# A hybrid encoder block whose modulation vectors are all made on the tensor engine in four column groups

## Chip, cores and metric

The kernel runs on one core of one Trainium2 chip. The metric is the device time of one execution in microseconds (us), the median over several runs. All data are float32 in device memory at the start and the end.

## What is computed

One block works on x (1024 tokens of 1024 channels) with a conditioning vector c of 1024 numbers. Six modulation vectors of 1024 numbers each come from c by one matrix:

```
c_act = silu(c)
mod = c_act @ ada_w + ada_b                      # 1024 x 6144
sh1, sc1, g1, sh2, sc2, g2 = split(mod, 6)
h = rmsnorm(x, norm1_g) * (1 + sc1) + sh1
p = h @ w_in                                     # S5 input, Hyena input, two sigmoid gates
merged = gate_a * (s5(p) @ w_branch_a) + gate_b * (hyena(p) @ w_branch_b)
x = x + g1 * (merged @ w_out)
h = rmsnorm(x, norm2_g) * (1 + sc2) + sh2
x = x + g2 * swiglu_ffn(h)
out = rmsnorm(x, final_g)
```

The S5 branch is a bidirectional scan over 32 groups; the Hyena branch makes two long convolutions with filters that a small network generates. The matrix `ada_w` has 1024 rows, which are the sum's index: eight tiles of 128 rows (partitions). It is 25 MB, the largest single weight that gives only a vector.

## The kernel before, in words

Python loops write out every instruction, and a scheduler then sets each engine's order once, from a model of the times: what comes earlier in the text has priority, and an instruction that is ready later is put behind others on its engine. On the chip every engine works through its list in that order and waits at semaphores. All loads and stores but a few go through one queue, that of SyncE (SP), in order too. Tiles come from pools; tiles with the same tag share a number of rooms (`bufs`), and a new tile waits until the older one in its room has been read for the last time.

The stages, with the time of the profiled execution:

- 0 to 50 us: constants, x (eight tiles of 128 tokens) and the first two vectors' part of `ada_w` (eight blocks of 1024 rows by 256 columns, `load_ada1`) are loaded; sums of squares (`emit_stats1`), the filter network (`emit_mlp`) and the vectors of the first norm (`emit_mod1`, L1080) are made. The order `ADA1 = (4, 0, 5, 1, 6, 2, 7, 3)` takes blocks of sc1 (4 to 7) and sh1 (0 to 3) by turns. A block of sc1 goes to PE: eight products with one column of silu(c) as the stationary operand and 128 x 256 of the weights moving (L1104), a float32 product being two passes in the trace, then a copy of one row (L1105). A block of sh1 is multiplied by silu(c) per partition and added over the eight row tiles: for one block on ACT and POOL (L1093, L1095), for three on DVE (L1097, L1099). What is left, a sum over 128 partitions, is made by 16 small products with ones (L1109, L1110), which also turn the row into columns (`E.mod`).
- 50 to 90 us: the normalised x is turned and modulated (`emit_norm1`: L1148 or L1150 makes a tile `hk`, L135 rounds it, L136 subtracts for the low part). The tag `hk` has two rooms, which the tiles `tt` of the turned convolutions (`emit_turn`, L1208) use as well.
- 57 to 345 us: the Hyena filters (`emit_filters`, four passes; L243 and L244 on PE, L247 on ACT, L250 and L255 on DVE, L256 on POOL), beside the projections of four convolution tiles (`emit_conv`, `proj`: each loads 512 KB of weights, ACT rounds, POOL subtracts, PE makes three products for each one of float32), the S5 inputs (`emit_u`) and later convolutions. Each pass loads one row `hb` (L227) that is added once (L252); it has a room of its own.
- In the same stretch `emit_ada` (L950) makes three more chunks of 1024 columns: 2 (g1), 4 (sc2) and 3 (sh2), each in two halves of 512 columns. For each half eight loads of 128 x 512 (256 KB) come through three rooms of a tile with tag `ax`; the first and the even tiles are multiplied and added on DVE (L962, L967), the odd ones are multiplied on ACT (L964) and added on POOL (L965). The bias row of chunk 2 is added on DVE (L972). The 128 partial sums go to device memory (`E.acc`, L973). The tag `ax` is used before by x tiles and after by a scratch tile of the S5 scan (`beside`).
- 345 to 640 us: S5 parameters and scan (`emit_s5`; L798, L877 on DVE, L807, L819, L856, L881 on PE), with the projections of the gates between. Then the GLU, the two long convolutions (to 900 us), the merge (`emit_merge`, to 965 us).
- In the merge `emit_ada_end` (L983) loads the partial sums back and adds over the partitions on PE: with ones on all columns where a vector is wanted along the free side (L992, g1 and g2), or turned to columns (`mod_columns`).
- 965 to 1080 us: the output projection (`emit_out`). After its first quarter of the second half of tokens, `between()` runs `last_gate`: chunk 5 (g2) by the same `emit_ada`, with two rooms for loads, and its `emit_ada_end`.
- to 1835 us: the feed-forward part, nearly all on PE; g2 is used there (L1417).

Of the kernel before, what the change touches and what calls it, by code (L numbers as in the profile page):

```python
# [15 lines left out]
L = 1024  # L16
# [139 lines left out]
def col(ap, i):  # L156
    return ap[:, i:i + 1]
# [45 lines left out]
def emit_filters(E):  # L203
    nc, d = E.nc, E.d
    sp = lambda: ps.tile([P, 2, 256], F32, tag="sp", name="sp", bufs=3)
    with ExitStack() as ctx:
        fp = ctx.enter_context(E.tc.tile_pool(name="flt", bufs=1, reuse_waits="tile"))
        ps = ctx.enter_context(E.tc.tile_pool(name="flt_ps", bufs=2, space=PSUM, reuse_waits="tile"))
        for o in range(2):
            for hf in range(2):  # L210
# [1 line left out]
                w3 = fp.tile([P, 2, 256], F32, tag="w3", name="w3")  # L212
                wd = fp.tile([P, 2, 256], F32, tag="fbt", name="wd", bufs=2)
                dec = fp.tile([P, 2, 256], F32, tag="dec", name="dec")
                hb = fp.tile([1, 256], F32, tag="hb", name="hb")
                col0 = o * 1024 + 256 * hf
                for s in range(2):
                    c = slice(col0 + 512 * s, col0 + 512 * s + 256)
# [519 lines left out]
def emit_s5(E, before):  # L738
# [5 lines left out]
    with ExitStack() as ctx:  # L744
# [1 line left out]
        ps = ctx.enter_context(E.tc.tile_pool(name="s5_ps", bufs=1, space=PSUM, reuse_waits="tile"))  # L746
        cs = op.tile([P, 8], F32, name="cs2")
        nc.scalar.activation(out=cs, in_=E.pf[:, PF_C:PF_C + 8], func=ACTF.Silu)
        nc.vector.tensor_copy(E.cs, cs)
        j8 = op.tile([P, 1, P], F32, name="j8")  # L750
        nc.sync.dma_start(out=j8[:, 0], in_=d["c_j8"])
        with E.tc.tile_pool(name="s5p", bufs=1, reuse_waits="tile") as pp:
# [183 lines left out]
def emit_setup(E, cp):  # L936

    nc = E.nc
    E.pf, E.pk = (cp.tile([P, n], F32, name=f"pk{n}") for n in (11, P))
    for rows, out in zip(E.rows, (E.pf, E.pk)):  # L940
        n = rows.shape[0]
        pt = E.mm.tile([P, n], F32, tag="mm", name="pkp")
        nc.tensor.transpose(pt, rows, E.ident[0:n, 0:n])
        nc.vector.tensor_copy(out, pt)
    E.cs = cp.tile([P, 8], F32, name="cs")
    nc.scalar.activation(out=E.cs, in_=E.pf[:, PF_C:PF_C + 8], func=ACTF.Silu)
    E.mod = cp.tile([P, 4, 8], F32, name="mod")


def emit_ada(E, chunks, sums, loads):  # L950


    nc = E.nc
    for q in chunks:
        for hf in range(2):
            acc = sums()
            for k in range(8):
                w = loads()
                c0 = L * q + 512 * hf
                nc.sync.dma_start(out=w, in_=E.d["ada_w"][0, P * k:P * k + P, c0:c0 + 512])  # L960
                if k == 0:
                    nc.vector.tensor_scalar(out=acc, in0=w, scalar1=col(E.cs, 0), scalar2=None, op0=ALU.mult)  # L962
                elif k % 2:
                    nc.scalar.mul(w, w, col(E.cs, k))  # L964
                    nc.gpsimd.tensor_tensor(out=acc, in0=acc, in1=w, op=ALU.add)  # L965
                else:
                    nc.vector.scalar_tensor_tensor(out=acc, in0=w, scalar=col(E.cs, k), in1=acc,  # L967
                                                   op0=ALU.mult, op1=ALU.add)
            if q in (2, 5):
                b = loads()[0:1]  # L970
                nc.sync.dma_start(out=b, in_=E.d["ada_b"][:, L * q + 512 * hf:L * q + 512 * hf + 512])
                nc.vector.tensor_tensor(out=acc[0:1], in0=acc[0:1], in1=b, op=ALU.add)  # L972
            nc.sync.dma_start(out=E.acc[q - 2, :, 512 * hf:512 * hf + 512], in_=acc)  # L973


def ada_rooms(E):

    t = [E.dft.tile([P, 4, 512], F32, tag="ax", name="ada")]
    loads = (t[0][:, 1 + i % 3] for i in range(1000))
    return lambda: t[0][:, 0], lambda: next(loads)  # L980


def emit_ada_end(E, psum, chunks, room):  # L983
# [95 lines left out]

def emit_mod1(E, ap, ps, blocks):  # L1080


    nc = E.nc
    V = nc.vector
    acc = ap.tile([P, L], F32, name="shacc")
    row = ap.tile([1, L], F32, name="scrow")
    for n, c in enumerate(ADA1):
        w = blocks[n]
        r = slice(256 * (c % 4), 256 * (c % 4) + 256)
        if c < 4:  # L1090
            for k in range(8):
                if n < 2:
                    nc.scalar.mul(w(k) if k else acc[:, r], w(k), col(E.cs, k))  # L1093
                    if k:
                        nc.gpsimd.tensor_tensor(out=acc[:, r], in0=acc[:, r], in1=w(k), op=ALU.add)  # L1095
                elif k == 0:
                    V.tensor_scalar(out=acc[:, r], in0=w(0), scalar1=col(E.cs, 0), scalar2=None, op0=ALU.mult)  # L1097
                else:
                    V.scalar_tensor_tensor(out=acc[:, r], in0=w(k), scalar=col(E.cs, k), in1=acc[:, r],  # L1099
                                           op0=ALU.mult, op1=ALU.add)  # L1100
        else:
            pt = ps.tile([1, 256], F32, tag="mrow", name="mrow")
            for k in range(8):
                nc.tensor.matmul(out=pt, lhsT=col(E.cs, k), rhs=w(k), start=k == 0, stop=k == 7)  # L1104
            nc.scalar.copy(row[:, r], pt)  # L1105
    pt = ps.tile([P, 16], F32, tag="mcol", name="mcol")
    for i in range(8):
        c = slice(P * i, P * i + P)
        nc.tensor.matmul(out=pt[:, i:i + 1], lhsT=acc[:, c], rhs=E.ones[:, 0:1], start=True, stop=True)  # L1109
        nc.tensor.matmul(out=pt[:, 8 + i:9 + i], lhsT=row[:, c], rhs=E.ones[0:1, 0:1], start=True, stop=True)  # L1110
    V.tensor_tensor(out=E.mod[:, 0:2].rearrange("p a b -> p (a b)"), in0=pt, in1=E.pk[:, PK_ADA:PK_ADA + 16], op=ALU.add)
    V.scalar_tensor_tensor(out=E.mod[:, 1], in0=E.mod[:, 1], scalar=1.0, in1=E.pk[:, PK_N1:PK_N1 + 8],
                           op0=ALU.add, op1=ALU.mult)
# [371 lines left out]
def hybrid_block(tc, d):  # L1485
# [4 lines left out]
    with ExitStack() as top:  # L1490
# [14 lines left out]
        with ExitStack() as s0:  # L1505
            E.h0 = pool(s0, "h0")
            E.dft = pool(s1, "dft")
            with ExitStack() as s2:
                E.cv = pool(s2, "cv")
                E.mm = pool(s2, "mmB", bufs=3, space=PSUM)  # L1510
                E.h1 = pool(s2, "h1")
                s3 = ExitStack()
                hhp = pool(s3, "hhp", side="right")
                E.hid, E.hid1 = (hhp.tile([P, 2, L], F32R, name=n) for n in ("hid", "hid1"))
                with ExitStack() as s4:
                    ada1 = pool(s4, "ada1", side="right")
                    mlp = pool(s4, "mlp", side="right")
                    ps = pool(s4, "st_ps", space=PSUM)
                    emit_consts(E, E.cp)
                    load_setup(E, mlp)  # L1520
                    E.x8, E.r1 = [], []
                    load_x1(E, range(4))
                    blocks = [load_ada1(E, ada1, n) for n in range(8)]
                    load_x1(E, range(4, 8))
                    emit_setup(E, E.cp)
                    for th in range(2):
                        emit_stats1(E, th)
                    emit_mlp(E, mlp, ps)
                    emit_mod1(E, ada1, ps, blocks)
                    emit_norm1(E)  # L1530
                emit_dft(E, E.cp)
                emit_filters(E)
                s3.close()
                for ct in range(4):
                    emit_conv(E, ct)
                emit_ada(E, (2, 4, 3), *ada_rooms(E))
                emit_s5(E, lambda: [emit_u(E, ct) for ct in range(4)])
                for ct in range(4, 12):
                    emit_conv(E, ct)
                emit_gates_a(E)  # L1540
                emit_glu(E)
            with ExitStack() as s2:
                E.gp = pool(s2, "gp")
                mm = pool(s2, "mmC", bufs=2, space=PSUM)
                emit_hyena(E, lambda: [emit_gates_b(E, mm), emit_branch_a(E, mm)])
            s1.close()
            mm = pool(top, "mmD", bufs=2, space=PSUM)
            pool(top, "edge", side="right").tile([P, 8], F32, name="edge")
            E.actT = pool(top, "actT", bufs=38, side="right")
            xp = pool(top, "x1", side="right")  # L1550
            rows = pool(top, "rows", side="right")
            E.g1, E.g2 = (rows.tile([P, L], F32, name=n) for n in ("g1", "g2"))
            woA = pool(wo, "woA", side="right")
            room = lambda t: xp.tile([P, L], F32, tag=f"x{t}", name="x1")
            x1 = [room(t) for t in range(4)]
            emit_merge(E, mm, x1, lambda c: c in (2, 4, 6) and
                       emit_ada_end(E, mm, ((2, 4, 3)[c // 2 - 1],), lambda n: room(3 + c // 2)))
        with ExitStack() as s0:
            ada2 = pool(s0, "ada2")
            x1 += [room(t) for t in range(4, 8)]  # L1560
            def last_gate():
                emit_ada(E, (5,), lambda: ada2.tile([P, 512], F32, tag="acc", name="acc"),
                         lambda: ada2.tile([P, 512], F32, tag="aw", name="aw", bufs=2))
                emit_ada_end(E, mm, (5,), lambda n: ada2.tile([P, L], F32, name="row"))
            emit_out(E, mm, x1, woA, last_gate)
        wo.close()
# [33 lines left out]
```

## Time and profile before

| | us |
|---|---|
| median of 3 runs | 1838.48 |
| lowest and highest run | 1837.70 and 1839.58 |
| the profiled execution | 1837.27 |
| its span, first to last instruction | 1835.5 |

The profiled execution is 1.77 us longer than its span (start and end of the program). Engines: PE multiplies, PEld loads its stationary operand, DVE is VectorE, ACT ScalarE, POOL GpSimd, SP the queue that issues transfers. A row of a group gives line, engine, operation, output and inputs by the program's names, shapes, count, then busy time in us and the mean of one in ns, then the idle time of the engine just before these instructions and what ended it. A row of waits gives who waited for whom, the sum in us, how often, and the longest.

### The profile page before, as it was taken

The numbers are of one execution on the slowest core, as the hardware profiler recorded it, in microseconds if no ns is written. First come the engines' busy times: TensorE is split into PE (matmuls) and PEld (weight loads), VectorE is DVE, ScalarE is ACT, GpSimd is POOL, SyncE is SP. The second block draws the span as 40 slices with busy tenths as digits, with TensorE's granted clock in tenths as the row PEclk, the third lists the DMA queues.
The fourth block names the chain that finished last, engine by engine and source line by source line (L and its number), as shares of the span: only waits on it lengthen the run. The fifth ranks groups of instructions, "written<-read, shape, count | busy, mean of one in ns | idle before, by whom it ended". The sixth has DMA issues, their size and how long they took to land.

```text
span 1835.5 us, 23003 instructions
## 1 busy us (share of the span) xinstructions
PE 1657.1 (90%) x8700; PEld 1401.9 (76%) x8700; DVE 1066.4 (58%) x1548; ACT 593.2 (32%) x1037; POOL 749.4 (41%) x509
## 2 busy tenths in 40 slices
PE   6778888987777898988699999999999999999996
PEld 2667777876666776767579978899888988899885
DVE  6889789779999637888877741123111321124127
ACT  5855454443333254122234531111111111110125
POOL 2356545258775347688511221212221222222234
PEclk9988999999888999999799999999999999999998
DMA  9446733523221357743277311111111111112112
GB/s 325 119 130 180 215 97 97 167 76 89 58 78 57 90 167 263 244 155 115 81 231 237 118 41 46 46 41 53 47 53 39 47 58 46 40 36 63 47 52 92
DMA packets 212946, 194.38 MB, mean 106 GB/s; under 512 B 23783, under 2 KB 174143, under 8 KB 211395
## 3 DMA queue, kind: packets, MB, share of 16 engines
q1 hardware_dynamic: 212356, 190.50, 33.7%
q0 software_dynamic: 480, 2.42, 0.4%
q8 instruction: 68, 1.11, 0.3%
q14 instruction: 42, 0.34, 0.1%
HBM read 149.91 MB, written 42.96 MB: 105 GB/s over the span
## 4 chain that ended last, share of the span: by engine, by line
PE 44%; DVE 3%; DMA 2%; ACT 1%; issue 0%; POOL 0%; ACTq 0%; SPq 0%; DVEq 0%; POOLq 0%
PE gu L144 9%; PE gu L146 9%; PE gu L145 9%; PE dn L146 4%; PE dn L144 4%; PE dn L145 4%; DMA wof<-in_w_out_dram 1%; PE wop L146 1%; PE wop L144 1%; PE wop L145 1%; PE br L144 1%; PE br L145 1%; PE br L146 1%; DVE x L1418 0%; DMA acc<-acc 0%
## 5 line engine op out<-in xcount | busy, mean ns | idle before, releaser
L136 POOL TENSOR_TENSOR wl<-wf,wh 128x1024 fp32r<-128x1024 f32 (+1 forms) x126 | 286.2, 2272 | 707.3 <-ACT wh L135 654.9
L135 ACT CAST wh<-wf 128x1024 fp32r<-128x1024 f32 (+1 forms) x126 | 118.3, 939 | 616.5 <-issue 196.2
L144 PE MATMUL gu<-h2T,wh 128*128 128x512 f32 x704 | 277.5, 396 | 3.4 <-ACT silu L1432 2.8
L145 PE MATMUL gu<-h2T,wh 128*128 128x512 f32 x704 | 278.6, 396 | 0.0
L146 PE MATMUL gu<-h2T,wl 128*128 128x512 f32 x704 | 278.4, 396 | 0.0
L1433 DVE TENSOR_TENSOR silu<-gu,silu 128x1024 f32<-128x1024 f32 x22 | 27.0, 1225 | 383.7 <-PE gu L146 377.3
L144 PE MATMUL pj<-hT,wh 128*128 128x512 f32 x480 | 196.5, 409 | 8.8 <-ACT cva L1180 8.1
L146 PE MATMUL pj<-hT,wl 128*128 128x512 f32 x480 | 195.0, 406 | 3.3 <-POOL wl L136 3.3
L146 PE MATMUL dn<-wh,act 128*128 128x256 f32 x576 | 162.6, 283 | 0.0
L145 PE MATMUL dn<-wl,act 128*128 128x256 f32 x576 | 162.6, 283 | 0.0
L144 PE MATMUL dn<-wh,act 128*128 128x256 f32 x576 | 161.5, 283 | 0.0
L144 PEld LDWEIGHTS gu<-h2T,wh 128*128 128x128 f32 x704 | 132.8, 189 | 35.2 <-ACT silu L1432 3.2
L146 PEld LDWEIGHTS gu<-h2T,wl 128*128 128x128 f32 x704 | 132.9, 189 | 31.2
L145 PEld LDWEIGHTS gu<-h2T,wh 128*128 128x128 f32 x704 | 133.0, 189 | 31.1
L144 PEld LDWEIGHTS pj<-hT,wh 128*128 128x128 f32 x480 | 94.9, 198 | 28.3 <-ACT cva L1180 8.8
L1417 DVE TENSOR_TENSOR tmp<-dn,g 128x256 f32<-128x256 f32 x96 | 36.0, 416 | 134.6 <-PE dn L146 134.6
L146 PEld LDWEIGHTS pj<-hT,wl 128*128 128x128 f32 x480 | 94.2, 196 | 23.0 <-POOL wl L136 4.2
L145 PEld LDWEIGHTS dn<-wl,act 128*128 128x128 f32 x576 | 110.6, 192 | 0.1
L146 PEld LDWEIGHTS dn<-wh,act 128*128 128x128 f32 x576 | 110.6, 192 | 0.0
L144 PEld LDWEIGHTS dn<-wh,act 128*128 128x128 f32 x576 | 109.9, 192 | 0.1
L145 PE MATMUL pj<-hT,wh 128*128 128x512 f32 x256 | 104.5, 408 | 0.0
L145 PE MATMUL pj<-lT,wh 128*128 128x512 f32 x224 | 90.1, 402 | 0.0
(411 smaller groups left out, 3733.8 us busy)
## 6 DMA issues: line engine op xcount, KB each, us to landing
wf<-in_ffn_w_gu_dram SPq DMA_DIRECT2D x44, 512.0 KB
wf<-in_w_in_dram SPq DMA_DIRECT2D x36, 512.0 KB
ada<-in_ada_w_dram SPq DMA_DIRECT2D x48, 256.0 KB
x<-in_x_dram SPq DMA_DIRECT2D x16, 512.0 KB
kt<-kspec SPq DMA_DIRECT2D x32, 256.0 KB
wof<-in_w_out_dram SPq DMA_DIRECT2D x16, 512.0 KB
wf<-in_ffn_w_down_dram SPq DMA_DIRECT2D x16, 512.0 KB
kspec<-kt SPq DMA_DIRECT2D x28, 256.0 KB
```

The lines of the kernel that those rows point to most:

```text
L135: E.nc.scalar.copy(hi, src)
L136: (lo_eng or E.nc.vector).tensor_tensor(out=lo, in0=src, in1=bc(hi), op=ALU.subtract)
L144: E.nc.tensor.matmul(out=out, lhsT=lh, rhs=rh, start=first, stop=False, skip_group_check=shared)
L145: E.nc.tensor.matmul(out=out, lhsT=lh, rhs=rl, start=False, stop=False, skip_group_check=shared)
L146: E.nc.tensor.matmul(out=out, lhsT=ll, rhs=rh, start=False, stop=last, skip_group_check=shared)
L1417: V.tensor_tensor(out=tmp, in0=acc, in1=E.g2[:, cs], op=ALU.mult)
L1433: V.tensor_tensor(out=s, in0=pts[1], in1=s, op=ALU.mult)
```

## The change

All chunks go through one function. `E.csx` holds silu(c) with 31 columns of zeros behind each of its eight columns, so that a stationary operand is 32 columns wide; the product with row tile k goes to partitions 32 (k mod 4) onwards of the result, so four groups of 32 output partitions take the eight row tiles by turns, two each. Rows 0, 32, 64 and 96 of the result hold the four partial sums, all other rows zeros; the sum over partitions with ones stays as it was. `emit_mod1` sends all its eight blocks this way. `emit_ada` works in 16 blocks of 256 columns, each loaded as 1 MB into the one room of `ax`; the result is copied by ACT to a tile of the tag `hk`, the bias goes to its row 1 by a transfer (chunks 2 and 5), and it is stored. Chunk 5 moves from the output projection to the other three. The filters' row `hb` moves to the tag `hk`.

```
-                hb = fp.tile([1, 256], F32, tag="hb", name="hb")
+                hb = E.cv.tile([1, 256], F32, tag="hk", name="hb", bufs=2)
...
-        nc.vector.tensor_copy(E.cs, cs)
...
-    E.cs = cp.tile([P, 8], F32, name="cs")
-    nc.scalar.activation(out=E.cs, in_=E.pf[:, PF_C:PF_C + 8], func=ACTF.Silu)
+    E.csx = cp.tile([P, 8, 32], F32, name="csx")
+    nc.vector.memset(E.csx, 0.0)
+    nc.scalar.activation(out=E.csx[:, :, 0], in_=E.pf[:, PF_C:PF_C + 8], func=ACTF.Silu)
...
+def matvec(E, pt, w):
+    for k in range(8):
+        g = slice(32 * (k % 4), 32 * (k % 4) + 32)
+        E.nc.tensor.matmul(out=pt[g], lhsT=E.csx[:, k], rhs=w(k), start=k < 4, stop=k >= 4)
...
-def emit_ada(E, chunks, sums, loads):
+def emit_ada(E, chunks):
     for q in chunks:
-        for hf in range(2):
...
+        for n in range(4):
+            c = slice(L * q + 256 * n, L * q + 256 * n + 256)
+            w = E.dft.tile([P, 8, 256], F32, tag="ax", name="ada")
+            nc.sync.dma_start(out=w, in_=d["ada_w"][0, :, c].rearrange("(k p) n -> p k n", p=P))
+            pt = E.mm.tile([P, 256], F32, tag="mm", name="mrow")
+            matvec(E, pt, lambda k: w[:, k])
+            acc = E.cv.tile([P, 256], F32, tag="hk", name="accr", bufs=2)
+            nc.scalar.copy(acc, pt)
             if q in (2, 5):
+                nc.sync.dma_start(out=acc[1:2], in_=d["ada_b"][:, c])
+            nc.sync.dma_start(out=E.acc[q - 2, :, 256 * n:256 * n + 256], in_=acc)
...
     for n, c in enumerate(ADA1):
...
+        pt = ps.tile([P, 256], F32, tag="mrow", name="mrow")
+        matvec(E, pt, blocks[n])
+        nc.scalar.copy(acc[:, 256 * c:256 * c + 256], pt)
     pt = ps.tile([P, 16], F32, tag="mcol", name="mcol")
+    for i in range(16):
+        nc.tensor.matmul(out=pt[:, i:i + 1], lhsT=acc[:, P * i:P * i + P], rhs=E.ones[:, 0:1], start=True, stop=True)
...
-                emit_ada(E, (2, 4, 3), *ada_rooms(E))
+                emit_ada(E, (2, 4, 3, 5))
...
             def last_gate():
-                emit_ada(E, (5,), lambda: ada2.tile([P, 512], F32, tag="acc", name="acc"),
-                         lambda: ada2.tile([P, 512], F32, tag="aw", name="aw", bufs=2))
                 emit_ada_end(E, mm, (5,), lambda n: ada2.tile([P, L], F32, name="row"))
```

## Rows read from the trace of the kernel before

**Rows 1.** The page's first part: busy us, share of the span, instructions.

```profile
PE 1657.1 (90%) x8700; PEld 1401.9 (76%) x8700; DVE 1066.4 (58%) x1548; ACT 593.2 (32%) x1037; POOL 749.4 (41%) x509
```

**Rows 2.** Table of windows: stretch in us, busy us, clock, DMA share, GB/s.

```profile
0.00:40.00 40.00, 24.68 (x98) 10.48 (x98) 25.25 (x55) 20.68 (x36) 12.92 (x18) 1.00 0.99 319
80.00:240.00 160.00, 133.81 (x670) 112.36 (x669) 138.79 (x180) 85.07 (x154) 94.06 (x62) 0.94 0.61 182
80.00:640.00 560.00, 466.17 (x2333) 390.69 (x2332) 487.33 (x692) 237.99 (x471) 321.75 (x232) 0.92 0.39 114
965.00:1080.00 115.00, 113.79 (x875) 108.79 (x874) 72.89 (x128) 50.63 (x110) 22.23 (x15) 1.00 0.46 149
```

In these rows the five busy times stand in the order PE, PEld, DVE, ACT, POOL.

**Rows 3.** Groups by line, 77 to 240 us: the sums of chunks 2, 4 and 3.

```profile
L965 POOL TENSOR_TENSOR ada<-ada 128x512 f32<-128x512 f32 x24 | 36.8, 1533 | 38.6 <-ACT ada L964 12.9 <-DVE ada L967 10.3 <-DVE ada L962 6.3
...
L967 DVE SCALAR_TENSOR_TENSOR ada<-ada,cs 128x512 f32<-128x512 f32 x18 | 18.5, 1026 | 6.4 <-POOL ada L965 6.4
...
L964 ACT ACTIVATE ada<-ada,cs 128x512 f32<-128x512 f32 x24 | 17.3, 720 | 25.8 <-DMA ada<-in_ada_w_dram 25.7
...
L972 DVE TENSOR_TENSOR ada<-ada 1x512 f32<-1x512 f32 x2 | 3.4, 1721 | 0.0
L962 DVE TENSOR_SCALAR ada<-ada,cs 128x512 f32<-128x512 f32 x6 | 3.0, 493 | 8.4 <-DMA acc<-ada 8.4
```

**Rows 4.** Waits of all engines, 77 to 240 us.

```profile
ACT ada L964 <- DMA ada<-in_ada_w_dram: 25.7, 14, 6.0
...
DVE ada L962 <- DMA acc<-ada: 8.4, 2, 6.0
...
DVE ada L967 <- POOL ada L965: 6.4, 5, 1.8
```

**Rows 5.** Waits of PE, 80 to 640 us, the three longest of 15.

```profile
PE kp L819 <- DVE cc L798: 21.4, 12, 5.1
PE yp L881 <- DVE M L877: 20.6, 8, 6.8
PE f L243 <- DVE fbt L250: 17.6, 6, 6.0
```

**Rows 6.** Groups by line on DVE, 20 to 50 us.

```profile
L1099 DVE SCALAR_TENSOR_TENSOR shacc<-aw,cs,shacc 128x256 f32<-128x256 f32 x21 | 10.9, 519 | 0.5
```

**Rows 7.** Timeline of DVE, 30 to 51 us: start us, us, instruction.

```profile
40.92 0.35 DVE L1097 TENSOR_SCALAR shacc<-aw,cs 128x256 f32<-128x256 f32 x1
...
45.69 1.53 DVE L1099 SCALAR_TENSOR_TENSOR shacc<-aw,cs,shacc 128x256 f32<-128x256 f32 x3
...
49.55 0.10 DVE L1112 SCALAR_TENSOR_TENSOR mod<-mod,pk 128x8 f32<-128x8 f32 x1
```

**Rows 8.** Timeline of PE, 16 to 34 us: start us, us of the passes together.

```profile
16.63 2.08 PE L191 MATMUL hps<-sin_h,w 128*128 128x512 f32 x2 [5.04 <-ACT sin_h L168]
18.63 1.97 PE L188 MATMUL hps<-feat,w 33*64 33x512 f32 x4
...
30.28 3.61 PE L1104 MATMUL mrow<-aw,cs 128*1 128x256 f32 x16 [1.32 <-ACT scrow L1105]
```

**Rows 9.** The tile hk: ns min/median/max, first and last start in us.

```profile
L135 ACT CAST hT<-hk x16: 601/612/622, 50.5 to 85.0; 128x512 fp32r<-128x512 f32 x16
...
L1150 DVE TENSOR_SCALAR hk<-xT,mod x8: 621/796/810, 49.7 to 81.7; 128x512 f32<-128x512 f32 x8
...
L136 DVE TENSOR_TENSOR lT<-hk,hT x8: 666/691/1802, 51.2 to 68.8; 128x512 fp32r<-128x512 f32 x8
```

**Rows 10.** Waits of PE, 940 to 1110 us.

```profile
PE modr L992 <- DMA row<-acc: 0.8, 1, 0.8
...
PE wop L144 <- DVE tmp L1373: 0.4, 1, 0.4
```

**Rows 11.** L255's group, 77 to 240 us; then L255 alone, ns min/median/max, whole span.

```profile
L255 DVE TENSOR_TENSOR ET<-fbt 128x256 f32<-128x256 f32 x18 | 17.6, 984 | 0.1
...
L255 DVE TENSOR_TENSOR ET<-fbt x32: 406/536/3418, 64.0 to 292.3; 128x256 f32<-128x256 f32 x32
```

More of the change, by code (lines that the diff above doesn't have):

```diff
@@ L944, in emit_setup @@
         nc.vector.tensor_copy(out, pt)
-    E.cs = cp.tile([P, 8], F32, name="cs")
-    nc.scalar.activation(out=E.cs, in_=E.pf[:, PF_C:PF_C + 8], func=ACTF.Silu)
+    E.csx = cp.tile([P, 8, 32], F32, name="csx")
+    nc.vector.memset(E.csx, 0.0)
+    nc.scalar.activation(out=E.csx[:, :, 0], in_=E.pf[:, PF_C:PF_C + 8], func=ACTF.Silu)
     E.mod = cp.tile([P, 4, 8], F32, name="mod")
-def emit_ada(E, chunks, sums, loads):
-    nc = E.nc
-    for q in chunks:
-        for hf in range(2):
[L956 to L968, printed above, removed]
-            if q in (2, 5):
[L970 to L973, printed above, removed]
@@ L976, in ada_rooms @@
[L976 to L980, printed above, removed]
+def matvec(E, pt, w):
[3 more added lines that the diff above has]
+def emit_ada(E, chunks):
+    nc, d = E.nc, E.d
+    for q in chunks:
+        for n in range(4):
[6 more added lines that the diff above has]
+            nc.scalar.copy(acc, pt)
+            if q in (2, 5):
+                nc.sync.dma_start(out=acc[1:2], in_=d["ada_b"][:, c])
+            nc.sync.dma_start(out=E.acc[q - 2, :, 256 * n:256 * n + 256], in_=acc)
@@ L1084, in emit_mod1 @@
     V = nc.vector
-    acc = ap.tile([P, L], F32, name="shacc")
-    row = ap.tile([1, L], F32, name="scrow")
+    acc = ap.tile([P, 2 * L], F32, name="modacc")
     for n, c in enumerate(ADA1):
[L1088 to L1105, printed above, removed]
+        pt = ps.tile([P, 256], F32, tag="mrow", name="mrow")
+        matvec(E, pt, blocks[n])
+        nc.scalar.copy(acc[:, 256 * c:256 * c + 256], pt)
     pt = ps.tile([P, 16], F32, tag="mcol", name="mcol")
[L1107 to L1110, printed above, removed]
+    for i in range(16):
+        nc.tensor.matmul(out=pt[:, i:i + 1], lhsT=acc[:, P * i:P * i + P], rhs=E.ones[:, 0:1], start=True, stop=True)
     V.tensor_tensor(out=E.mod[:, 0:2].rearrange("p a b -> p (a b)"), in0=pt, in1=E.pk[:, PK_ADA:PK_ADA + 16], op=ALU.add)
```

## The prediction

> **What bounds the kernel now.** I read the page's busy times first. PE is busy 90% of the span [rows 1], so it looks like the bound, but that is an average over stages, and the table of windows tells them apart [rows 2]. From 965 us on PE hardly rests (113.8 of 115 us), so nothing done for another engine can pay there. From 80 to 640 us (filters, first projections and convolutions, the S5 scan) PE works 466.2 of 560 us and DVE 487.3: here PE loses 94 us, and DVE is the fuller engine. This is the stretch in which three of the four late modulation chunks are made, and the fourth moves into it.
>
> Next, the groups of that stretch that belong to the modulation sums [rows 3]: DVE 18.5 + 3.0 + 3.4 = 24.9 us, ACT 17.3 us, POOL 36.8 us. Then who waited [rows 4]: DVE stood 8.4 us before a product whose sum tile was still being stored, and 6.4 us for POOL's half of the sum, 14.8 us together; ACT stood 25.7 us, 14 times, for the 256 KB loads. These engines work in order, so whatever is queued behind such a product waits too. Last, what PE waited for between 80 and 640 us [rows 5]: 21.4 and 20.6 us for DVE inside the S5 scan (with smaller ones there, some 54 us) and 17.6 us for a filter product of DVE (with smaller ones, some 39 us before 345 us). So the chain of the early half runs through DVE, and PE's idle time there is DVE's lateness.
>
> **The first part: the vectors of the first norm.** Removed are 24 products on DVE, 21 of which took 10.9 us [rows 6], eight on ACT and seven sums on POOL; added are four more blocks on PE. DVE is busy without a pause while it makes the last block's sums, from 40.92 to 47.2 us, and the vectors are ready at 49.65 us [rows 7]. The load of that block must be earlier: 40 us at 319 GB/s [rows 2] is 12.8 MB, and about 11.9 MB are issued up to its end (four x tiles, eight 1 MB blocks, constants), so I estimate its landing at 37.4 us. With PE's 1.1 us (below), a copy of 0.5 us and the 2.4 us that today lie between the last sum and the vectors, they are ready at about 41.4 us: 8 us early at most. I take 5 us, since the filters' inputs and the norm's second half have other chains; ends 0 and 8.
>
> **What a block costs on PE.** Today's block is eight fp32 products in 16 passes, 3.61 us one behind the other [rows 8]. In the change four groups of 32 columns go by turns. No row shows four. Two groups of 64 columns are there: four passes of 512 columns took 1.97 us right behind two full-width passes of 512 columns that took 2.08 us [rows 8], so two column groups do run beside each other, and the change of shape left no gap. Bounds: 3.61 us (nothing overlaps) and 0.9 us (a quarter). I take 1.1 us, near the quarter, as two groups overlapped fully. The 16 late blocks then add 18 us to PE between 80 and 640 us; ends 14 and 58.
> The Trainium skill, TensorE: Matmul & The Clock Gate, "Measured speedup vs the span model", has three column tiles at 2.38 times, not three. By that figure a block is an estimated 1.5 us, the 16 are 24 us, and the sum below ends near 1822 us; no run here shows it yet.
>
> **The middle part: chunks 2, 4, 3 and 5.** DVE gets back 24.9 us of work and up to 14.8 us of waiting, 39.7 us in all. PE sets a second limit: of its 94 idle us, 54 belong to the scan, where nothing is changed, and 18 go to the new blocks. What is left, 22 us, is the gain if every one of PE's waits before 345 us goes. I take 16 us; ends 0 and 39.7. ACT has 17.3 us of products less and 16 copies of about 0.5 us more; it is not full, so I cost that at nothing (0.5 us: a 512-column product takes 0.72 [rows 3]). Its cover is room on ACT; if that were gone, 8 us.
>
> Four smaller things. **Loads**: 16 of 1 MB in place of 48 of 256 KB, through a room that holds one. Each load is issued after the last product on the block before it, so SP waits for PE, with projection weights and filter stores queued behind. Today SP waits there for DVE and POOL instead, so I cost SP at nothing. On PE, arriving before the load means a wait, with projections queued behind it; ACT today pays 25.7 / 24 = 1.1 us a load [rows 4], which for 16 would be 18 us if all of it reached the chain. Ends 0 and 18 (a gain is already in the 14.8); I take the 6 us that stand off the 22. **Issues**: 16 loads, 16 stores and 8 bias rows (chunks 2 and 5) take the place of 48, 6 and 2 on SP, fewer in all; the chunk that moves adds 4.2 MB to a stretch where DMA is 0.61 full [rows 2], which covers it; if not, 13 us at 319 GB/s. **Rooms**: the bias row of the filters and the 16 result tiles now share two rooms with the first norm's tiles and the turned tiles. If the bias row sits in one, the first norm has the other alone: its 16 tiles go at (85.0 - 50.5) / 15 = 2.3 us each now [rows 9], and a tile's own chain (make 0.8, round 0.61, subtract 0.69) is 2.1 us, so I take nothing; ends 0 and 5. A result with a bias row holds its room for two landings in turn, and the next copy waits; behind that copy on ACT stand the filters' exponentials. The sums are not read before the merge near 900 us, so lateness alone costs nothing. **The fourth chunk out of the last projection**: PE waited there 0.8 us for its sum and 0.4 us for a DVE product [rows 10]. I take 1 us, ends 0 and 2: the chain's path through those loads is no gain, because PE was busy beside them.
>
> Sum against the profiled execution: 1837.3 - 5 - 16 - 1 = 1815.3 us. The median of the runs is 1.2 us above that execution, so 1816 us.
>
> **The rivals.**
> *DVE is the only limit.* If PE's projections fill the scan's gaps, the 54 us are not fixed, and the whole 39.7 us arrive: 1837.3 - 5 - 39.7 - 1 + 1.2 = 1793 us. For it: the scan has PE idle. POOL beside DVE would add to this: the 18 sums of the filters in this stretch average 984 ns, against 406 at their shortest [rows 11], an excess of 18 x 0.578 = 10.4 us, and POOL's modulation work is 36.8 of its 94.1 us [rows 2, 3], so some 4 us more, 1789 us. The Trainium skill, SBUF — State Buffer, "SBUF: two separate sides", has DVE and GpSimd lock one port pair against each other for a whole instruction; the spread from 406 to 3418 ns agrees, and by that rule alone 36.8 us of POOL's would be an upper end of what DVE gets back on top. Against the whole case: PE works in a written order, and its scan waits are for DVE results. Chance 0.12.
> *The relief goes nowhere.* PE's waits move to other producers (the POOL halves of the split weights, ACT's exponentials) and take up the first part's 5 us too, so that only the 1 us of the last projection arrives: 1837.3 - 1 + 1.2 = 1837.5 us, no change. For it: a wait on PE has many causes before 345 us, of which the largest makes 17.6 of 39 us. Chance 0.12.
> *PE waits for its loads* (the slower side). One room means load, products, load, one after another. A 1 MB load at 319 GB/s is 3.3 us; if PE stands before each of the 16, that is 53 us. PE's idle 39 us of that stretch hide as much of it, 14 us do not, and DVE's relief is lost behind them: + 14 in place of - 16, so 1837.3 - 5 + 14 - 1 + 1.2 = 1846 us. It decides from 22 / 16 = 1.4 us a load, where the gain is gone. For it: ACT's 1.1 us a load today. Against: PE is behind, not ahead, in this stretch. Chance 0.14.
> *The groups don't overlap.* The blocks take 3.61 us, 58 us in the middle; 466 + 58 + 54 = 578 us of PE in 560, + 18, and the first part gives nothing: 1837.3 + 18 - 1 + 1.2 = 1855 us. Against: the 1.97 us. Chance 0.08.
>
> **How the numbers follow.** The forecast has 0.54, with a range of its own of 1804 to 1828 us. A measurement of this kernel tells 0.2% (3.7 us) from no change. Faster: 0.54 + 0.12 = 0.66; same 0.12; slower 0.14 + 0.08 = 0.22. The range goes from 1789 us (DVE alone, with POOL's share) to 1846 us (load waits); the serial case lies outside.
>
> **What would show it.** Right: the blocks' 16 passes span about 1 us; the first vectors stand at 41 to 45 us; PE's wait for the filter product shrinks from 17.6 us; the scan ends some 20 us before 640; from the last projection on the trace is the old one, moved. Wrong: PE waits before the new blocks for the loads above 1.4 us each; blocks of 3 us; the scan's end unmoved although DVE is emptier before it.

## The result, and the profile after

Before 1838.09 us, after 1909.84 us (medians of 4 runs each): ratio 1.0395, 95% interval 1.0363 to 1.0426. The change makes the kernel 3.9% **slower**; forecast were 1816 us, and the range ended at 1846. The profiled execution took 1907.71 us, its span 1905.9.

First the page's busy line and the windows of the kernel after, with the columns of [rows 1, 2] (five busy times as PE, PEld, DVE, ACT, POOL, then clock, DMA share, GB/s):

```profile
PE 1689.6 (89%) x9020; PEld 1419.5 (74%) x9020; DVE 986.5 (52%) x1488; ACT 576.8 (30%) x1017; POOL 687.3 (36%) x470
...
0.00:40.00 40.00, 24.03 (x174) 10.74 (x174) 19.85 (x45) 22.04 (x37) 4.01 (x11) 1.00 0.99 325
80.00:240.00 160.00, 117.11 (x683) 93.33 (x682) 132.22 (x208) 81.80 (x162) 65.46 (x48) 0.81 0.43 138
80.00:640.00 560.00, 423.64 (x2242) 344.63 (x2242) 434.06 (x667) 225.00 (x449) 267.00 (x200) 0.85 0.38 111
640.00:742.10 102.10, 102.10 (x452) 84.59 (x451) 0.00 (x0) 21.34 (x30) 25.22 (x11) 1.00 0.30 102
```

DVE was relieved: 434.1 us busy between 80 and 640 instead of 487.3. But PE, which was to profit, did less there, 423.6 instead of 466.2, at a mean granted clock of 0.85 instead of 0.92 [rows 2]. The missing work comes after: from 640 to 742 us PE works without a gap and DVE not at all. The groups of that stretch are only projections (pj), the gates that used to fill the scan.

A landmark makes this a sum. The long convolutions begin with the load of their first input tile, T, which is behind all projections and the gated unit. Up to it, PE's time is products and idle time. The first group of lines is the kernel before, the second after (windows from 80 us to that load, then 180 to 300 us):

```profile
80.00:673.20 593.20, 496.06 (x2455) 414.52 (x2454) 496.10 (x696) 257.25 (x489) 334.24 (x236) 0.92 0.40 116
...
180.00:300.00 120.00, 103.35 (x542) 87.04 (x542) 102.32 (x134) 61.46 (x114) 63.25 (x45) 0.99 0.51 151
```
```profile
80.00:742.10 662.10, 525.75 (x2692) 429.23 (x2692) 434.06 (x667) 246.33 (x479) 292.22 (x211) 0.87 0.37 109
...
180.00:300.00 120.00, 66.23 (x454) 44.35 (x454) 84.38 (x189) 45.49 (x100) 32.79 (x30) 0.69 0.63 205
...
742.10:1096.10 354.00, 315.98 (x1579) 266.71 (x1579) 274.73 (x344) 110.18 (x216) 187.49 (x143) 0.95 0.52 176
```

T is 68.9 us later: 29.7 us more products (525.75 - 496.06) and 39.2 us more idle time (136.3 against 97.1). From there to the second norm's first rounded tile (`h2T`) it is 354.0 us, before 354.9 (T at 673.2, `h2T` at 1028.1); the rest is 2.4 us longer. So 68.9 of the 70.4 us of span come from ahead of T, and the worst stretch is 180 to 300 us, where PE works 66 of 120 us, before 103.

DVE's relief up to T is 62.0 us (496.10 - 434.06), more than twice the 24.9 us of products that were taken from it: other work of DVE became shorter too, the 26 sums of L255 alone by 9.7 us (22.1 to 12.4).

What PE did there: the first rows are PE's waits, 80 to 640 us as in [rows 5]. Then come the timeline of SP's loads for the blocks and of the blocks on PE, the blocks as a group, and the copies of the S5 inputs from PE (`us`; min/median/max ns, first and last start), the last row that of the kernel before:

```profile
PE mrow L955 <- DMA ada<-in_ada_w_dram: 37.4, 10, 9.5
...
PE f L243 <- ACT w3h L231: 13.8, 2, 8.8
...
PE f L243 <- DVE fbt L250: 5.5, 4, 1.7
```
```profile
206.25 0.37 SPq L965 DMA_DIRECT2D ada<-in_ada_w_dram  x1
...
213.69 0.38 SPq L965 DMA_DIRECT2D ada<-in_ada_w_dram  x1
...
221.35 0.38 SPq L965 DMA_DIRECT2D ada<-in_ada_w_dram  x1
...
204.40 1.81 PE L955 MATMUL mrow<-ada,csx 128*32 128x256 f32 x16 [1.10 <-DMA ada<-in_ada_w_dram]
...
211.69 1.94 PE L955 MATMUL mrow<-ada,csx 128*32 128x256 f32 x16 [1.16 <-DMA ada<-in_ada_w_dram]
...
219.37 1.94 PE L955 MATMUL mrow<-ada,csx 128*32 128x256 f32 x16 [1.87 <-DMA ada<-in_ada_w_dram]
...
L955 PE MATMUL mrow<-ada,csx x256: 376/633/637, 168.4 to 297.4; 128*32 128x256 f32 x128
...
L1191 ACT COPY us<-pj x8: 578/587/589, 304.8 to 347.8; 128x512 f32<-128x512 f32 x8
```
```profile
L1218 ACT COPY us<-pj x8: 564/574/589, 170.9 to 240.7; 128x512 f32<-128x512 f32 x8
```

Load, products, load: each load is issued when the products on the one before are over, its own products start mostly some 5.5 us later, and the 16 blocks go from 168.4 to 297.4 us, one every 8.5 us on average. In all that time PE's list holds, beside the blocks, hardly anything but products of the filters. The projections of the S5 inputs, copied from 170.9 us on before, are copied from 304.8 us on, 7 us behind the last block. PE's wait for the filter product did shrink (5.5 us; 17.6 before [rows 5]), as forecast; a wait of 13.8 us for `w3h`, the filters' weights, is nearly new (0.8 before).

**Theory** from this trace: the 16 result tiles take the three result rooms (tag `mm`) of the projections, and rooms are given in the order of the text. The projections written behind the blocks therefore cannot pass them, however long a load takes. Rivals: PE's waits for loads alone (A); the blocks, their copies or the shared rooms of the tag `hk` (B); the scheduler's priority (C).

### The profile page after: what moved, and what is told of

The parts are those of the page before. It is cut to its first block, busy times and chain, and to the rows that moved or that the text cites. A ratio compares the mean times of both kernels' runs of the same rounds, so it can differ in the third digit from the quotient of the medians.

```text
span 1905.9 us, 23404 instructions
## 1 busy us (share of the span) xinstructions
PE 1689.6 (89%) x9020; PEld 1419.5 (74%) x9020; DVE 986.5 (52%) x1488; ACT 576.8 (30%) x1017; POOL 687.3 (36%) x470
## 5 line engine op out<-in xcount | busy, mean ns | idle before, releaser
L136 POOL TENSOR_TENSOR wl<-wf,wh 128x1024 fp32r<-128x1024 f32 (+1 forms) x126 | 281.2, 2232 | 785.3 <-ACT wh L135 731.7
L144 PE MATMUL pj<-hT,wh 128*128 128x512 f32 x480 | 197.6, 412 | 8.3 <-ACT wh L135 5.4
L146 PEld LDWEIGHTS pj<-hT,wl 128*128 128x128 f32 x480 | 94.5, 197 | 20.6 <-POOL wl L136 0.3
```

The costliest lines, as they stand in the source:

```text
L136: (lo_eng or E.nc.vector).tensor_tensor(out=lo, in0=src, in1=bc(hi), op=ALU.subtract)
L144: E.nc.tensor.matmul(out=out, lhsT=lh, rhs=rh, start=first, stop=False, skip_group_check=shared)
L146: E.nc.tensor.matmul(out=out, lhsT=ll, rhs=rh, start=False, stop=last, skip_group_check=shared)
```

## The experiments

Ratios are to runs of the kernel before on the same chip.

**One load for all blocks** (chunks 2, 4, 3 and 5 get the first block's weights, so the vectors are others):

```
+            if (q, n) == (chunks[0], 0):
...
                 w = E.dft.tile(...); nc.sync.dma_start(out=w, ...)
```


> The kernel after with one load of 1 MB in place of 16: all 16 late blocks multiply the first block's weights, so the vectors of chunks 2, 4, 3 and 5 are not the reference's. Theory (the blocks stand ahead of the later projections in the text, share three rooms with them, and come one load at a time, so the projections start only when the 16th load has been used): without the chain of loads the 16 blocks are through PE in some 30 us instead of 129, the S5 inputs start near 230 us instead of 305, and the kernel comes to 1815 to 1835 us. Rival A (it is only PE's 70 us of standing before the loads): 1909.8 - 70 = 1840 us, with the S5 inputs still started near 300 us less the 70. Rival B (the blocks themselves, their copies or the shared rooms of the tag hk are what costs): 1890 us or more.


1836.76 us, 0.9996 (0.9986 to 1.0006). 73 us are gone; S5 inputs from 218 us, idle time ahead of T 92.4 us. So the chain of loads carries the loss, and B falls as the main cause. Theory and A lie too close for this run to part them (1.8 us over the one's upper end, 3 under the other's).

**Priority for the projections, the text unchanged:**

```
+                at = tc.cur_priority
                 emit_ada(E, (2, 4, 3, 5))
...
+                    with tc.high_priority(tc.cur_priority - at):   # around emit_u and emit_conv 4 to 11
```


> The kernel after with the S5 inputs and convolution tiles 4 to 11 given a higher priority than the 16 blocks; their place in the text, and with it the order in which rooms are handed out, stays. Theory (rooms are handed out in the order of the text): the S5 inputs still start near 305 us, and the time stays within 1% of 1909.8 us, 1895 to 1920. Rival C (the scheduler prefers the blocks because they come first or are thought cheap): the projections move ahead of the blocks, 1815 to 1840 us.


1877.98 us, 1.0219 (1.0202 to 1.0236), below the band: a miss in size. But the S5 inputs start at 306.4 us, as the theory has it and against C: priority does not carry a projection past the blocks. The 32 us come later. With the convolution tiles ahead of the scan PE is busy 79.9 of 80 us from 320 to 400 us (62.1 in after).

**The blocks spread in the text**, one behind each half projection:

```
         yield slice(512 * th, 512 * th + 512), pt
+        next(E.ada, None)
```


> The kernel after with the 16 blocks spread in the text: one behind each half projection of convolution tiles 0 to 3 and of the S5 inputs (8 + 8 halves). Loads, products, copies and rooms are the same. Theory: a load of some 5.5 us is hidden behind the 24 products of a half projection (5.5 us) and nothing is postponed, so what the prediction forecast arrives, 1810 to 1830 us, and PE's gate projections no longer run alone after 640 us. Rival A (each load costs PE its wait wherever the block stands): 1840 to 1870 us. Rival B (the blocks' copies, the two shared rooms or the moved chunk cost): 1890 us or more.


1866.58 us, 1.0163 (1.0148 to 1.0178): 43 us better than after by the place in the text alone, but far from 1820. The time lies in A's band, but PE's wait for these loads is down to 5.7 us, so what is left is not A's wait. What stays is idle time of 107.5 us ahead of T: 14.0 us for ACT's convolution tiles and 10.9 us for `w3h`. The latter led to the next runs; this run still has `hb` in the shared rooms.

**The first part alone**, with the bias row `hb` in the shared rooms as in after, and then **with `hb` in its own room**, in the kernel before and in after. For the 1 KB of room, silu(c) is stored with 17 columns from one value to the next, and an operand is a window of 32:

```
-                hb = E.cv.tile([1, 256], F32, tag="hk", name="hb", bufs=2)
+                hb = fp.tile([1, 256], F32, tag="hb", name="hb")
...
-    E.csx = cp.tile([P, 8, 32], F32, name="csx")
+    E.csx = cp.tile([P, 151], F32, name="csx")
...
-        lhsT=E.csx[:, k]
+        lhsT=E.csx[:, 17 * k:17 * k + 32]
```


> The kernel before with only the first part changed: all eight blocks of the first norm's vectors by the four column groups (and the filters' bias row in the shared rooms, as after); chunks 2, 4, 3 and 5 as before. Theory: the first part is a gain of its own, vectors at 43.8 us instead of 49.6, and the early half stays as in the kernel before, 1830 to 1836 us. Rival D (the shared rooms of the bias row hold up the first norm or the filters): 1840 us or more. Rival E (the early half absorbs it): 1837 to 1839 us.


1848.11 us, 1.0064 (1.0042 to 1.0087): rival D. T comes at 683.8 us, 10.6 later than before.


> The kernel before with the first part changed alone, and hb in its own room as before. e4_first_part, with hb shared, took 1848 us, 10 us over before. Theory: those 10 us and the 5 us of the first part were both there and the shared room ate them; with the own room 1829 to 1836 us, and no wait of PE for w3h. Rival E (PE's work up to the gated unit is the bound, and an earlier start of the filters only lengthens its waits there): 1836.5 to 1840 us. Rival F (the blocks of the first part on PE cost more than they save): 1843 us or more.


1841.78 us, 1.0023 (1.0014 to 1.0032): 6 us back, but not below before; it lies between the bands of E and F. T is 3.4 us earlier (669.8); the long convolutions lose more than that, where PE's wait for a product of DVE is 8.0 us instead of 4.9.


> The kernel after with the filters' bias row hb back in a room of its own (to make place, the eight columns of silu(c) stand 17 apart in one row of 151 with zeros between, and a stationary operand is a window of 32 over it; the products stay the same). Theory, second half: in the two shared rooms hb's load waits for the first norm's and the turned tiles, SP holds every later load behind it, and PE stands 14 us (28 with the weight loads) before w3h; with its own room this wait is gone and the kernel comes to 1882 to 1898 us, still far above before, since the chain of blocks is untouched. Rival B (the rooms cost nothing beside the chain): 1903 to 1915 us.


1880.7 us, 1.0233 (1.0218 to 1.0249): **29 us for one row of 1 KB**, 1 us below the theory's band. Rows of the tile `hb` (loads, readings, SP's wait before a load) and of the copies of turned tiles (`tt`), of after and then of this run:

```profile
L227 SPq DMA_DIRECT2D hb<-in_hy_bias_dram x4: 223/242/250, 79.8 to 103.4; - x4
L252 DVE TENSOR_TENSOR fbt<-fbt,hb x4: 349/406/942, 83.2 to 197.6; 1x256 f32<-1x256 f32 x4
...
SPq L227 <- DVE fbt L252: 10.1, 1, 10.1
...
146.22 0.94 DVE L252 TENSOR_TENSOR fbt<-fbt,hb 1x256 f32<-1x256 f32 x1
...
147.87 0.58 ACT L1182 COPY tt<-tp 128x512 f32<-128x512 f32 x1
```
```profile
L227 SPq DMA_DIRECT2D hb<-in_hy_bias_dram x4: 223/236/315, 50.3 to 157.6; - x4
...
SPq L227 <- DVE fbt L252: 9.9, 1, 9.9
...
L1182 ACT COPY tt<-tp x16: 575/591/656, 111.5 to 446.1; 128x512 f32<-128x512 f32 x16
...
PE f L243 <- ACT w3h L231: 3.2, 1, 3.2
```

The wait for `w3h` goes from 13.8 to 3.2 us. The theory's reason, SP held up by the row's load, does not show: SP's longest wait before such a load is 10.1 us with the shared room and 9.9 with its own, all of them from 45 to 110 us 14.6 and 13.3. What differs is how long a row holds its room. It takes the room at its load and gives it back when it is read. In after the third row is loaded at 87.4 us and read at 146.2, the fourth loaded at 103.4 and read at 197.6; so from 103.4 to 146.2 us these two, written ahead of all turned tiles, hold both rooms. PE makes the first transposed tile in a result room from 103.9 us on, and its copy to `tt` starts at 147.9 us, right behind the third reading. With the own room such copies start at 111.5 us, and from 103.9 to 147.9 us PE works 39.2 us instead of 31.1. In five of the six kernels with the shared room the first `tt` comes 1.5 to 1.7 us behind the third reading (which is at 145.6 to 167.4 us), in the interleaved one later still, in those with the own room at 111 to 118 us. How the 29 us add up from there was not tested.

**Two half loads by turns** in the one room:

```
...
+            for i in range(2):
...
+                nc.sync.dma_start(out=w[:, i], ...)       # 128 columns, 512 KB
+                matvec(E, pt[:, P * i:P * i + P], lambda k: w[:, i, k])
```


> The kernel after with each load cut in two halves of 128 columns (512 KB), which take the two halves of the same room by turns, so that one half loads while the other is multiplied. Order of the text, rooms for results and hb as in after. Theory (the chain load, products, load paces the blocks at 8 us each and postpones the projections by its length): about 5 to 6 us a block in place of 8, so 30 to 50 us less, 1860 to 1880 us, S5 inputs from 260 to 275 us. Rival B (the length of the chain does not matter): within 1% of 1909.8 us.


1889.92 us, 1.0275 (1.0259 to 1.0291). The right direction, half the size: 20 us, between the theory's band and rival B's, whose edge it misses by 1 us. The blocks go from 168.6 to 277.2 us, so the chain is 20 us shorter, 1.3 us a block; S5 inputs from 280.0 us.

**A result room for the blocks, and its control.** This is the run that decides. In both kernels the projections have two result rooms instead of three, `hb` has its own, and a block's result is copied into its own weights tile. In the control the third bank is held empty; in the other the blocks use it. Nothing else differs:

```
-            pt = E.mm.tile([P, 256], F32, tag="mm", name="mrow")
+            pt = E.mr.tile([P, 256], F32, tag="mrow", name="mrow")
```


> Control for g1_own_rooms. f1_hb with the shared result rooms cut from three to two (the third bank is held but not used), and the copy of a block's result going into the block's own weights tile instead of the tag hk. Blocks, projections and turned tiles still take the two result rooms in the order of the text. Theory: the S5 inputs start behind the 16th block as before, at 280 to 320 us; 1875 to 1915 us.

> The same as g0_two_rooms, but the result of a block goes to the held bank, a room of its own. Text, loads, products, copies and the number of rooms for everything else are those of g0. Theory (what postpones the projections is the turn for the shared result rooms, given in the order of the text): the S5 inputs start near 170 to 200 us though the 16 blocks still come one load after the other, and the kernel is 25 to 60 us below g0, 1835 to 1865 us. Rival H (they are postponed by anything else: the priority that comes with the place in the text, the load queue, the room for weights): S5 inputs at 280 us or later and the time within 1% of g0.


The control took 1936.18 us, 1.0548 (1.052 to 1.0576); with the room 1841.5 us, 1.0017 (1.0008 to 1.0026). The control is slower than its band by 21 us (its blocks last from 152.8 to 326.9 us, a longer chain than with three rooms), the difference of 95 us is over what was expected, and rival H is out. Against the kernel with `hb` in its own room and three shared result rooms (1880.7 us) the extra room brings 39 us. S5 inputs and windows, control first:

```profile
L1191 ACT COPY us<-pj x8: 574/583/589, 334.2 to 375.8; 128x512 f32<-128x512 f32 x8
...
80.00:759.20 679.20, 522.64 (x2705) 427.51 (x2704) 430.27 (x665) 246.64 (x479) 287.93 (x210) 0.86 0.36 108
180.00:300.00 120.00, 59.26 (x387) 42.53 (x386) 79.70 (x172) 42.75 (x93) 35.67 (x29) 0.64 0.51 170
...
PE mrow L955 <- DMA ada<-in_ada_w_dram: 61.8, 10, 9.6
```
```profile
L1191 ACT COPY us<-pj x8: 567/582/635, 165.8 to 233.0; 128x512 f32<-128x512 f32 x8
...
80.00:667.80 587.80, 511.39 (x2704) 416.53 (x2703) 449.97 (x665) 244.83 (x479) 297.92 (x210) 0.94 0.43 125
180.00:300.00 120.00, 113.62 (x667) 90.07 (x666) 92.21 (x134) 61.14 (x120) 49.72 (x36) 0.99 0.60 182
```

The loads still come one behind the other, the blocks last until 360 us, and it no longer matters: the projections start at 165.8 us, PE works 113.6 of the same 120 us instead of 59.3, and its granted clock there is 0.99 instead of 0.64. But this kernel is no faster than before. Its T comes 5.4 us earlier (667.8): PE's idle time ahead of T is 20.7 us less (76.4 against 97.1), and its products take 15.3 us more (511.39 - 496.06).

**The blocks behind the scan**, beside the long convolutions (results in the rooms of the branch's projection), `hb` in its own room; then the same with more priority for convolution tiles, and with the first part of the kernel before:

```
-                emit_ada(E, (2, 4, 3, 5))
...
             nc.sync.dma_start(out=E.ya[c, :, r], in_=g)
+            next(ada)                       # in emit_branch_a: one block behind each half tile
```


> The 16 blocks moved in the text behind the scan: one behind each half tile of the first branch's projection, beside the long convolutions, where PE has room (18 of 100 us idle in 840 to 940 us before) and nothing waits behind them but that projection; hb in its own room. Loads, products and sums are those of after. Theory: DVE's relief in the filters and the first part stay, the chain and some 20 to 30 us of blocks leave the stretch where PE is the bound, 1800 to 1825 us. Rival G (16 MB more in a stretch where DMA is up to 0.68 full holds up the long convolutions' loads, or the blocks stop the branch's projection): 1835 to 1860 us. Rival E (PE's waits in the early half grow by what DVE gives back): 1828 to 1840 us.


1818.91 us, 0.9892 (0.9876 to 0.9909): **1.1% faster than before**, the best of all.

```profile
80.00:646.70 566.70, 486.39 (x2440) 407.94 (x2439) 452.39 (x666) 240.50 (x464) 300.30 (x210) 0.93 0.34 97
...
646.70:1009.20 362.50, 331.35 (x1835) 269.52 (x1834) 278.12 (x344) 116.12 (x231) 184.47 (x143) 0.97 0.67 222
...
PE mrow L955 <- DMA ada<-in_ada_w_dram: 3.3, 5, 1.6
```

T comes at 646.7 us, 26.5 earlier than before. The stretch to the second norm's `h2T` takes 362.5 us, 7.6 longer, for 16 blocks; rival G's contention is in that at most.


> f5_late (1818.9 us) with convolution tiles 4 to 11 put ahead of the S5 parameters and scan in priority. In e2_prio such a change went with 32 us less than after, and PE hardly idle in 320 to 400 us. Theory: in f5_late the projections are no longer held up, so there is nothing to catch up and the order decides little, 1812 to 1825 us. Rival: PE's waits inside the scan are what is left (80 us of idle before the long convolutions), and more projections earlier leave fewer to fill them, 1826 us or more; or fewer idle us, 1810 us or less.


1829.77 us, 0.9952 (0.9937 to 0.9967): slower than without, the first half of the rival. Idle time ahead of T is 94.0 us, against 80.3; PE waits 29.1 us for DVE's M, against 20.2.


> f5_late (1818.9 us) with the first part as in the kernel before: the vectors of the first norm by elementwise products and sums on DVE, ACT and POOL again, four blocks of eight on PE with one column each. The 16 late blocks stay as in f5_late. Theory (the first part brings the vectors some 5 us earlier, and once the room of hb is its own again this reaches the early half): 1820 to 1826 us, first vectors near 49 us. Rival E (the early half absorbs an earlier start): 1816 to 1820 us. Rival F (four blocks more on PE cost more than they give): 1815 us or less.


1826.97 us, 0.9935 (0.9915 to 0.9954), 1 us over the theory's band; T at 652.6 us. The first part is worth 5.9 us at T and some 8 us at the end.

```profile
80.00:652.60 572.60, 491.24 (x2455) 411.98 (x2454) 457.58 (x669) 241.21 (x465) 301.53 (x212) 0.93 0.35 98
```

## Why the prediction was wrong

Point by point, by its own steps.

**The first part, -5: right.** The vectors stand at 44.7 us (timeline of DVE in after, where before has 49.65 [rows 7]):

```profile
44.62 0.10 DVE L1085 SCALAR_TENSOR_TENSOR mod<-mod,pk 128x8 f32<-128x8 f32 x1
```

Taken out of the best kernel they cost 5.9 us at T. In the kernel before, alone, they brought 3.4 us at T, and the end came 4 us later: a gain early is not yet a gain.

**What a block costs on PE, 1.1 us: right at full clock, short at the lower.** Timeline of PE, a block of the first part and a late one in after:

```profile
24.93 1.07 PE L955 MATMUL mrow<-aw,csx 128*32 128x256 f32 x16
...
211.69 1.94 PE L955 MATMUL mrow<-ada,csx 128*32 128x256 f32 x16 [1.16 <-DMA ada<-in_ada_w_dram]
```

Four groups by turns take 1.07 us where the serial block took 3.61 [rows 8], 3.4 times. The Trainium skill, TensorE: Matmul & The Clock Gate, "Measured speedup vs the span model", gives 2.38 times for three column tiles. Four do better here, and the 1.5 us a block estimated from it were too long. But most late blocks ran while PE stood waiting between them, at the level of 1.2 GHz (granted clock 0.50 from 211.69 to 213.60 us, on average 0.69 from 180 to 300), and took 1.9 us: 27.6 us in all instead of 18. The term was sized at a clock that the change itself took away. Where PE has work between the blocks, as in the kernel with the blocks behind the scan, every block whose passes run together takes 1.07 us again.

**The middle part, -16: the direction right, the sum not met where the blocks are in that stretch.** The kernel with the late blocks and the old first part has the relief alone: PE's idle time ahead of T falls from 97.1 to 81.4 us, 15.8 us, the same number of products takes 4.8 us less, and T is 20.6 us earlier. That the 15.8 meet the 16 is in part luck: the 16 were what stays after 18 us for the blocks and 6 us for the loads, and here both are gone from the stretch. With the blocks there and a result room of their own (and one room less for the projections), T came 5.4 us earlier, the first part's 5 us included; of the net 16 us nothing is left there.

**The step that failed** is in the four smaller things, under Rooms: "The sums are not read before the merge near 900 us, so lateness alone costs nothing." It looked at who reads the results, not at who needs the rooms next. The result rooms on the PE side, where the 16 blocks take turns with every projection written behind them, were not counted at all; only the copies' rooms were. Measured by one extra bank: 95 us between control and kernel, where the projections have two rooms, and 39 us against three shared ones. The term Loads had the pace of this chain at 6 us, 18 at most; in after itself the chain carries 73 us.

The same step sized the shared room of `hb` at 0 to 5 us by the chain of the norm's tiles. It measured 29 us in after and 6 in the kernel with the first part alone. The norm's tiles lost nothing, as it said (the last is rounded from 79.9 us, with the own room from 81.0). But it priced only them, not the turned tiles, which come behind the rows for the same two rooms and wait until the third row is read.

**The rival on the slower side, PE waits for its loads,** named the right place and the right condition: it decides from 1.4 us a load, and PE's waits were 37.4 / 16 = 2.3 us. Its price, 1846 us, was too low for the same reason: it took PE's idle 39 us as cover and the projections as there to fill. "Against: PE is behind, not ahead, in this stretch" is true only while PE has projections to be behind with. It also priced a load at 3.3 us; from its issue to its first product it took 5.3 us and more. The waits as such are not the whole loss: 37.4 us against the 73 that one load saves. The run with its own result room has 1.4 us of them, beside other work.

**Loads and issues at nothing** on SP: nothing in the runs points to their number. **The last projection, -1:** there. Its products go from 968.0 to 1067.7 us before and from 1038.3 to 1135.4 in after, 99.7 against 97.1 us, and the two waits of [rows 10] are gone. What follows is 2.7 us longer in after; why was not tested.

**DVE is the only limit:** DVE got back 62.0 us up to T, more than the 39.7 of this rival, and the kernel became slower. So DVE was not the only limit.

The chain of reason ran: DVE relieved, so PE waits less, so the projections end earlier. Each link shows in the kernels without the late blocks in that stretch, but the change put 16 slow steps into the one order in which PE gets its filling work. The Trainium skill, Perfetto Trace Analysis, "Optimization Strategy", reads a gap that repeats on the engine that should be saturated as possibly too little room for the next tile. Two rooms were short here: the single one for weights sets the rhythm of 8.5 us, and the shared result rooms keep projections out of its gaps. The extra bank shows the second. It could have been read before: the kernel gives three result rooms to everything from `emit_norm1` to `emit_glu`.

Open: what the interleaved order would give with `hb` in its own room (not tried); why the kernel with the extra result room stays 25 us above the forecast; and why a kernel that reaches T 3 to 5 us earlier loses 6 to 10 us behind it (first part alone, own result room). PE's wait in the long convolutions for one product of DVE is 8 to 13 us there instead of 5; but it is 8.0 us in after as well, where that stretch took no longer, and the cause was not tested.

## What to carry to other kernels

When work moves to an engine, follow not only its time there but the rooms that its results take, and who stands behind it for the same rooms in the text: a step paced by a one-room load makes everything behind it wait at that pace. Give such a step its own room, or place it where nothing that fills the bound engine is written behind it. A row of 1 KB cost 29 us here by sharing two rooms: what counts is not its size but the time from its load to its last reading, and who waits for the room meanwhile.

## What was not expected

Four column groups overlapped more fully than two rows of before could show (1.07 us against 3.61). The clock nearly doubled the price of a block: it took 1.07 us among dense work and 1.94 us among waits, and with a result room for the blocks the granted clock of 180 to 300 us went from 0.64 to 0.99.
